# Weights of v in layer 0: high part by casting loads, low part by adding loads, for units 2 to 15

## The chip, the cores and the metric

The kernel runs on one core of one Trainium2 chip. The metric is the device time of the whole program in microseconds (us). Before the change it is 1315.11 us, the median of three runs (1314.94 to 1315.18).

## What is computed

A two-layer encoder step for 512 prompt rows and 8 x 16 sample rows, 640 token rows of 1024 in all, in float32. Layer 0 is a gated MLP, layer 1 an attention with forgetting. What the change touches is one product of layer 0, the v part of the input projection:

```python
h = rms_norm(x, norm_pre[0])                 # 640 x 1024
proj = h @ gmlp_w_in[0]                      # 1024 x 6144: u | v | z, 2048 columns each
uv = gelu(proj[..., :4096]); z = proj[..., 4096:]
v = layer_norm(uv[..., 2048:], ln_g, ln_b)
s = einsum('gij,bnjgc->bnigc', masked_w_s, v) + b_s
y = u * s * silu(z)                          # then y @ w_out, norms, embeddings, layer 1
```

## The kernel before

**Split operands.** TensorE multiplies in a reduced float32 form (fp32r). To keep float32 accuracy each operand is held as two fp32r parts, high = the rounded value and low = value minus high, and each product is three matmuls (`mm3`, lines 258 to 260): high by high, high by low, low by high. `split` makes the two parts: ScalarE copies into the high part (line 272), VectorE subtracts it from the source for the low part (line 273).

**Units of weights.** All weights of the program are cut into units of 512 KB, in the order of use. A unit of v is 256 rows by 512 columns: two blocks of 128 x 512. The 2048 columns of v are four panels p of 512 columns, each with four units kk (256 of the 1024 rows each), so units 0 to 15 are the weights of v and unit 4p + kk belongs to panel p. `fetch` loads a unit into one of three RAW buffers by a DMA on SyncE's queue (SP); `prefetch` gives each unit one of five slots of the tile W (2048 numbers per partition: 1024 high, 1024 low), splits it there and so fills W as far ahead as free slots allow. A slot is free again when TensorE has used its unit with all five token tiles. `weights(n)` hands out the next units and prefetches.

**The v stage.** For each panel five PSUM banks collect the five token tiles t (128 rows each); each unit is multiplied with the five tiles (5 x 2 x 3 = 30 matmuls of 128x512). At a panel's end ScalarE applies gelu (line 460) and VectorE takes statistics (line 461). After panel 3 the stage of u and z follows, whose units go through other sums (`left_operands`, line 200, on GpSimd, POOL in the profile).

**The start.** Ten loads bring the 640 token rows x; for each tile ScalarE squares one half (line 380), VectorE the other (381), VectorE adds (384, 280), GpSimd takes the power -0.5 (`rstd_of`, line 282), VectorE scales the rows (388), TensorE transposes them (296) and `split` writes the tile A, TensorE's other operand. Meanwhile units 0 to 4 are fetched and split.

**What sets the order.** The kernel is written with a tile framework whose scheduler orders each engine's instructions by its own timeline; each engine then runs its list strictly in order, and an instruction that waits for a semaphore holds all behind it on that engine. A DMA issued by GpSimd stands in GpSimd's list like any instruction. Semaphores come from the data that instructions read and write.

Of the kernel before, what the change touches and what calls it, by code (L numbers as in the profile page):

```python
# [19 lines left out]
AF = mybir.ActivationFunctionType  # L20
ALU = mybir.AluOpType
# [36 lines left out]
def hybrid_trunk(tc, x_prompt, x_sample, ck, cv, clf, p_prompt, p_sample, norm_pre, norm_post,  # L58
                 g_win, ln_g, ln_b, w_s, b_s, g_wout, f_win, b_f, f_wout, w_proj, w_gate, consts,
                 y_p, y_s, st_v, fk_p, fv_p, fl_p, fk_s, fv_s, fl_s):  # L60
    nc = tc.nc
# [28 lines left out]
    def r1(o, n, p=P):  # L90
        return R1[:p, o:o + n]

    def f(ap):
        return ap.bitcast(F32)
# [8 lines left out]
    def bank(lst=(0, 1, 2, 3, 4, 5, 6, 7)):  # L103
        return PB[ring(("bank", lst), lst)]
# [13 lines left out]
    def dma(out, in_):  # L118
        behind["sp"] = nc.sync.dma_start(out=out, in_=in_)
# [10 lines left out]
    units = []  # L130
# [12 lines left out]
    def u_tail(wout, layer):  # L143
        for h in range(2):
            for kk in range(8):
                u_rows(wout[0], kk * 256, h * 512, 2, 512)
        for h in range(2):
            u_rows(w_proj[layer], 0, h * 512, 2, 512)
        for h in range(2):
            for kk in range(4):  # L150
                u_rows(w_gate[layer], kk * 256, h * 512, 2, 512)

    u_tail(g_wout, 0)
    joined = set()
    for p in range(8):
        for part in (2, 1, 0, 3):
            for kk in range(2):
# [18 lines left out]
    state = {"raw": 0, "used": 0}  # L176

    def raw_of(i):
        if S0 <= i < S1:
            z = (i - S0 + 1) % 4  # L180
            if z == NRAW:
                return r1(o_X, 1024)
        else:
            z = i % NRAW if i < S0 else (i + 1) % NRAW
        return RAW[:, z * 1024:z * 1024 + 1024]

    def fetch(upto):
        while state["raw"] < min(upto, len(units)):
            ap, k = units[state["raw"]]
            dma(raw_of(state["raw"]).rearrange("p (k n) -> p k n", k=k), ap)  # L190
            state["raw"] += 1

    def left_operands(i, j):

        (a11, a21), (a12, a22) = ([raw_of(r).rearrange("p (k n) -> p k n", k=4)[:, :, z:z + P] for z in (0, P)] for r in (i, i + 1))
        s2, s3, s1, s4 = (SF[:, z * 512:z * 512 + 512].rearrange("p (k n) -> p k n", k=4) for z in range(4))
        if j == 0:
            for o, a, b, op in ((s1, a21, a22, ALU.add), (s2, s1, a11, ALU.subtract), (s3, a11, a21, ALU.subtract),
                                (s4, a12, s2, ALU.subtract)):
                nc.gpsimd.tensor_tensor(out=o, in0=a, in1=b, op=op)  # L200
        return (a11, SF[:, :1024], SF[:, 1024:2048], raw_of(i + 1))[j]

    def prefetch(upto, i0=0):

        while len(place) < min(upto, len(items)):
            i = len(place)
            u, j = items[i]
            taken = {z for k in range(i0, i) for z in place[k]}
            step = 1 if j == 0 else 2
            free = [z for z in range(0, 2 * (NW - (u in few)), step) if not taken & set(range(z, z + step))]  # L210
            if not free:
                return
            z = min(free, key=lambda z: max(last_use[z:z + step]))
            place.append(range(z, z + step))
            last_use[z:z + step] = [i] * step
            fetch(u + 1 if j is None else u + 2)
            o, n = z * 1024, step * 512
            hi, lo = W[:, o:o + n], W[:, o + n:o + 2 * n]
            if u in joined:
                k = units[u][1]  # L220
                hi, lo = (W[:, o:o + 2 * n].rearrange("p (k z n) -> p z k n", z=2, k=k)[:, z] for z in range(2))
                split(hi, lo, raw_of(u).rearrange("p (k n) -> p k n", k=k))
            elif j is None:
                split(hi, lo, raw_of(u))
            else:
                split(*((x.rearrange("p (k n) -> p k n", k=4) for x in (hi, lo)) if j == 0 else (hi, lo)), left_operands(u, j))
                if u > S0:
                    fetch(u + 4)

    def weights(n):  # L230

        i0 = state["used"]
        state["used"] += n
        prefetch(i0 + 2 * NW, i0)
        res = []
        for i in range(i0, i0 + n):
            u, j = items[i]
            k, o, m = units[u][1], place[i][0] * 1024, len(place[i]) * 512
            if u in joined:
                res.append(W[:, o:o + 2 * m].rearrange("p (k n) -> p k n", k=k))  # L240
                continue
            if j in (1, 2):
                views = [W[:, o + z:o + z + m].rearrange("p (a k n) -> p k a n", a=2, k=k) for z in (0, m)]
            else:
                views = [W[:, o + z:o + z + m].rearrange("p (k n) -> p k n", k=k) for z in (0, m)]
            res.append(tuple(views))
        return res
# [22 lines left out]
    def split(hi, lo, src):  # L270

        nc.scalar.activation(out=hi, in_=src, func=AF.Copy)  # L272
        nc.vector.tensor_tensor(out=lo, in0=src, in1=f(hi), op=ALU.subtract)  # L273
# [77 lines left out]
    def r2(o, n, p=P):  # L351
        return R2[:p, o:o + n]
# [13 lines left out]
    for i in range(N_WARM):  # L366
        nc.tensor.matmul(PB[7][:, :256], warm[:, :P], warm[:, 256:], start=True, stop=True)
    fetch(1)
    for t in range(1, NT):
        for h in range(2):  # L370
# [6 lines left out]
    for t in range(NT):  # L377
        x, xn = r2(t * D, D), r2(5120 + (t % 2) * D, D)
        ss = [small(), small()]
        nc.scalar.activation(out=xn[:, :512], in_=x[:, :512], func=AF.Square, accum_out=ss[0])  # L380
        nc.vector.scalar_tensor_tensor(out=xn[:, 512:], in0=x[:, 512:], scalar=1.0, in1=x[:, 512:], op0=ALU.mult, op1=ALU.mult,
                                       accum_out=ss[1])
        sq = small()
        nc.vector.tensor_tensor(out=sq, in0=ss[0], in1=ss[1], op=ALU.add)
        rs = rstd_of(sq, RMS_EPS)
        for h in range(2):
            hs = slice(h * 512, (h + 1) * 512)
            nc.vector.scalar_tensor_tensor(out=xn[:, hs], in0=x[:, hs], scalar=rs, in1=gb[h], op0=ALU.mult, op1=ALU.mult)
        transposed_split(xn, lambda c: h_hi[:, 4 * c:4 * c + 4, t * P:(t + 1) * P],
                         lambda c: h_lo[:, 4 * c:4 * c + 4, t * P:(t + 1) * P], (5, 6, 7))  # L390
        prefetch(t + 1)
# [51 lines left out]
    for p in range(4):  # L443
# [3 lines left out]
        out = [bank((0, 1, 2, 3, 4, 5, 6, 7)) for _ in range(NT)]  # L447
        for kk in range(4):
            (w,) = weights(1)
            for t in range(NT):  # L450
                for j in range(2):
                    k = 2 * kk + j
# [318 lines left out]
    n = NT * H  # L771
# [55 lines left out]
    scale = DH ** -0.5  # L827
# [343 lines left out]
```

## Time and profile before

| | |
|---|---|
| Median of three runs | 1315.11 us |
| Profiled execution | 1315.17 us, its span (first to last instruction) 1313.4 us |
| TensorE busy | 1304.7 us, 99% of the span |
| VectorE, ScalarE, GpSimd busy | 794.1, 553.1, 136.1 us |
| Mean granted TensorE clock | 0.997 of full speed |
| HBM read, written | 149.86 MB, 21.59 MB |
| v stage: last gelu of panels 0, 1, 2, 3 starts | 45.14, 71.89, 99.86, 127.43 us |

Times in the rows are microseconds from the first instruction. In a row of the timeline stand start, length, engine, line, operation, what it writes and reads, and in brackets how long the engine had been idle and what ended that. SPq and POOLq are the queues of DMA issues of SyncE and GpSimd.

### The profile page before, as it was taken

How to read it: one execution, taken by the hardware profiler on the slowest of the kernel's cores; microseconds unless marked ns; L12 is line 12 of the kernel's file. 1: busy time of each engine (PE TensorE's matmuls, PEld its weight loads, DVE VectorE, ACT ScalarE, POOL GpSimd, SP SyncE). 2: the span in 40 equal slices, each digit the busy share in tenths (PEclk: the TensorE clock that was granted, in tenths of full speed). 3: DMA queues.
4: the chain of work that ended last, by engine and by line, in shares of the span. 5: the costliest groups of instructions: out<-in, count | busy, mean ns of one | idle time of the engine just before them, and what ended most of it. 6: DMA issues, size and time to landing. Idle time of an engine off the chain costs nothing.

```text
span 1313.4 us, 20355 instructions
## 1 busy us (share of the span) xinstructions
PE 1304.7 (99%) x7683; PEld 1152.3 (88%) x7683; DVE 794.1 (60%) x1671; ACT 553.1 (42%) x1074; POOL 136.1 (10%) x144
## 2 busy tenths in 40 slices
PE   8999999999999999999999999999999999999998
PEld 6888999999988888888999889898988988888887
DVE  7744999999844455644555554556555566554543
ACT  5334555444535343533433334333434344435431
POOL 1012454543000000000000000000000000000100
PEclk8999999999999999999999999999999999999999
DMA  6432333232424213589676665788557687343211
GB/s 227 132 108 67 120 118 121 86 104 73 129 94 149 79 49 113 167 135 149 152 194 151 155 160 148 165 150 171 132 150 163 149 213 235 113 132 132 66 56 57
DMA packets 300053, 172.79 MB, mean 132 GB/s; under 512 B 188785, under 2 KB 269473, under 8 KB 299954
## 3 DMA queue, kind: packets, MB, share of 16 engines
q1 hardware_dynamic: 299810, 171.23, 49.3%
q8 instruction: 60, 0.98, 0.3%
q14 instruction: 39, 0.32, 0.1%
q10 hardware_dynamic: 144, 0.26, 0.1%
HBM read 149.86 MB, written 21.59 MB: 131 GB/s over the span
## 4 chain that ended last, share of the span: by engine, by line
PE 95%; DVE 3%; DMA 1%; issue 1%; ACT 0%; SPq 0%; POOL 0%; DVEq 0%
PE pb L258 22%; PE pb L260 22%; PE pb L259 22%; PE pb L324 7%; PE pb L867 6%; PE pb L325 3%; PE pb L868 3%; PE pb L986 3%; PE pb L979 1%; PE pb L1040 1%; PE pb L1066 1%; PE pb L296 1%; DVE W L273 1%; PE pb L571 1%; PE pb L1063 1%
## 5 line engine op out<-in xcount | busy, mean ns | idle before, releaser
L273 DVE TENSOR_TENSOR W<-RAW,W 128x1024 fp32r<-128x1024 f32 (+1 forms) x156 | 193.5, 1242 | 170.8 <-ACT W L272 136.5
L272 ACT ACTIVATE W<-RAW 128x1024 fp32r<-128x1024 f32 (+1 forms) x156 | 161.0, 1033 | 151.0 <-PE pb L260 47.5
L258 PE MATMUL pb<-A,W 128*128 128x384 f32 (+1 forms) x640 | 221.8, 347 | 0.0
L260 PE MATMUL pb<-A,W 128*128 128x384 f32 (+1 forms) x640 | 208.7, 326 | 0.0
L259 PE MATMUL pb<-A,W 128*128 128x384 f32 (+1 forms) x640 | 208.3, 325 | 0.0
L258 PE MATMUL pb<-W,A 128*128 128x512 f32 x520 | 205.0, 395 | 2.3 <-ACT A L272 2.3
L259 PE MATMUL pb<-W,A 128*128 128x512 f32 x520 | 203.7, 392 | 0.0
L260 PE MATMUL pb<-W,A 128*128 128x512 f32 x520 | 203.3, 393 | 0.1
L324 PE MATMUL pb<-A,W 128*128 128x512 f32 x384 | 150.7, 393 | 0.0
L258 PEld LDWEIGHTS pb<-A,W 128*128 128x128 f32 x640 | 120.4, 188 | 18.7 <-issue 8.9
L259 PEld LDWEIGHTS pb<-A,W 128*128 128x128 f32 x640 | 121.0, 189 | 0.7
L260 PEld LDWEIGHTS pb<-A,W 128*128 128x128 f32 x640 | 120.2, 188 | 0.1
L258 PEld LDWEIGHTS pb<-W,A 128*128 128x128 f32 x520 | 98.1, 189 | 22.3 <-ACT A L272 2.5
L867 PE MATMUL pb<-W,A 128*128 128x512 f32 x320 | 116.6, 403 | 0.0
L260 PEld LDWEIGHTS pb<-W,A 128*128 128x128 f32 x520 | 97.9, 188 | 20.9 <-DVE A L273 0.6
L259 PEld LDWEIGHTS pb<-W,A 128*128 128x128 f32 x520 | 98.0, 188 | 19.4
L325 PE MATMUL pb<-A,W 128*128 128x256 f32 x384 | 107.7, 280 | 0.0
L868 PE MATMUL pb<-W,A 128*128 128x256 f32 x320 | 89.5, 280 | 0.0
L273 DVE TENSOR_TENSOR A<-R,A 128x640 fp32r<-128x640 f32 (+1 forms) x51 | 41.0, 836 | 71.4 <-ACT A L272 70.7
L867 PEld LDWEIGHTS pb<-W,A 128*128 128x128 f32 x320 | 60.0, 188 | 15.1 <-DVE R L872 2.6
L325 PEld LDWEIGHTS pb<-A,W 128*128 128x128 f32 x384 | 72.1, 188 | 0.4 <-issue 0.4
L324 PEld LDWEIGHTS pb<-A,W 128*128 128x128 f32 x384 | 72.1, 188 | 0.2
(252 smaller groups left out, 2285.8 us busy)
## 6 DMA issues: line engine op xcount, KB each, us to landing
RAW<-in_fox_w_in SPq DMA_DIRECT2D x64, 512.0 KB
RAW<-in_gmlp_w_in SPq DMA_DIRECT2D x40, 512.0 KB
r2b_t<-in_cache_fox_v SPq DMA_DIRECT2D x32, 512.0 KB
r2b_t<-in_cache_fox_k SPq DMA_DIRECT2D x128, 128.0 KB
RAW<-in_gmlp_w_out SPq DMA_DIRECT2D x16, 512.0 KB
RAW<-in_ple_w_gate SPq DMA_DIRECT2D x16, 512.0 KB
RAW<-in_fox_w_out SPq DMA_DIRECT2D x16, 512.0 KB
out<-R SPq DMA_DIRECT2D x42, 128.0 KB
```

Of the source, the lines that this page charges most:

```text
L258: nc.tensor.matmul(out, lh, rh, start=start, stop=False)
L259: nc.tensor.matmul(out, lh, rl, start=False, stop=False)
L260: nc.tensor.matmul(out, ll, rh, start=False, stop=stop)
L272: nc.scalar.activation(out=hi, in_=src, func=AF.Copy)
L273: nc.vector.tensor_tensor(out=lo, in0=src, in1=f(hi), op=ALU.subtract)
L296: nc.tensor.transpose(out=b[:, j * P:(j + 1) * P], in_=src[:, (4 * c + j) * P:(4 * c + j + 1) * P], identity=ident)
L324: nc.tensor.matmul(out[1].rearrange("p (z n) -> p z n", z=2), w[0], h_both[:, :, k, SA:], start=k == 0, stop=False)
L325: nc.tensor.matmul(out[1][:, :TOK - SA], w[1], h_hi[:, k, SA:], start=False, stop=k == 7)
L571: nc.tensor.matmul(b0[:, t * P:(t + 1) * P], v_at(pnl, t)[:, c0:c0 + P], wm, start=True, stop=True)
L867: nc.tensor.matmul(b, hi, w, start=k == 0, stop=False)
L868: nc.tensor.matmul(b[:, :256], lo, w[:, :256], start=False, stop=k == 7)
L986: nc.tensor.matmul(O[:, d], v[:, j, hh * P:(hh + 1) * P], pt[:, j * P:(j + 1) * P], start=(j == 0), stop=(j == i))
```

## The change

For units 2 to 15 `fetch` loads nothing into RAW. Instead `prefetch` issues a load from GpSimd that goes straight from the weights in HBM to the unit's high half in W, cast to fp32r on the way; ScalarE writes the negative of the high part into the low half; a second load from GpSimd reads the same weights again and adds them to the low half. Units 0 and 1, and all from 16 on, are split as before. So 14 loads of 512 KB on SP's queue, 14 copies on ScalarE and 14 subtractions on VectorE (128x1024 each) go; 28 loads of 512 KB on GpSimd's queue and 14 negating copies on ScalarE (128x1024) come.

```diff
-    joined = set()
+    joined, by_dma = set(), set(range(2, 16))
...
     def fetch(upto):
         while state["raw"] < min(upto, len(units)):
+            if state["raw"] in by_dma:
+                state["raw"] += 1
+                continue
             ap, k = units[state["raw"]]
...
                 split(hi, lo, raw_of(u).rearrange("p (k n) -> p k n", k=k))
+            elif u in by_dma:
+                src, k = units[u]
+                hi, lo = (x.rearrange("p (k n) -> p k n", k=k) for x in (hi, lo))
+                nc.gpsimd.dma_start(out=hi, in_=src)
+                nc.scalar.activation(out=lo, in_=f(hi), func=AF.Copy, scale=-1.0)
+                nc.gpsimd.dma_start(out=lo, in_=src, accum_op=ALU.add)
             elif j is None:
                 split(hi, lo, raw_of(u))
```

The change shifts line numbers by 9 behind the new code: line 282 is 291 in the changed kernel, 380 is 389, 272 is 281, 499 is 508; line 200 is 203. The new lines are 229 (casting load), 230 (negation) and 231 (adding load).

GpSimd at the start, before (line 282 is the power; the row ISA ahead of it selects GpSimd's library; line 499 clears two blocks; line 200 is `left_operands`):

```order
L1167 UNCONDITIONAL_BRANCH
L282 ISA
L282 TENSOR_TENSOR SML<-SML 128x1 x5
L499 MEMSET R_69 64x64 x2
L200 TENSOR_TENSOR sf<-RAW 128x512 x2
L200 TENSOR_TENSOR sf<-sf,RAW 128x512
```

And now:

```order
L1176 UNCONDITIONAL_BRANCH
L229 DMA W<-in_gmlp_w_in 128x2x512 x3
L231 DMA W<-in_gmlp_w_in 128x2x512
L291 ISA
L291 TENSOR_TENSOR SML<-SML 128x1
L231 DMA W<-in_gmlp_w_in 128x2x512 x2
L291 TENSOR_TENSOR SML<-SML 128x1 x4
```

The casting loads of units 2, 3 and 4 stand first, the adding load of unit 2 ahead of the power of tile 0, and those of units 3 and 4 ahead of the power of tile 1.

ScalarE at the start, before (line 380 squares a tile of x, line 272 copies a high part, into W for a weight and into A for a transposed tile):

```order
L380 ACT_TABLE_LOAD
L380 ACTIVATE r2a_t,SML<-r2a_t 128x512
L272 ACTIVATE W<-RAW 128x1024
L380 ACTIVATE r2a_t,SML<-r2a_t 128x512
L272 ACTIVATE A<-pb_75 128x4x128
L380 ACTIVATE r2a_t,SML<-r2a_t 128x512
L272 ACTIVATE W<-RAW 128x1024
L272 ACTIVATE A<-pb_76 128x4x128
```

And now:

```order
L230 ACT_TABLE_LOAD
L230 ACTIVATE W<-W 128x1024
L389 ACTIVATE r2a_t,SML<-r2a_t 128x512
L230 ACTIVATE W<-W 128x1024
L281 ACTIVATE W<-RAW 128x1024
L281 ACTIVATE A<-pb_75 128x4x128
L389 ACTIVATE r2a_t,SML<-r2a_t 128x512
L281 ACTIVATE A<-pb_76 128x4x128
L230 ACTIVATE W<-W 128x1024
```

The negation of unit 2 stands ahead of the first square, that of unit 3 ahead of the split of unit 0, and that of unit 4 behind both halves of tile 0. On TensorE 9 matmuls and 20 transposes now stand ahead of the first matmul that needs the low part of unit 1 (before, 7 and 16); from unit 5 on its order is the same in both.

GpSimd further on, now (before, only line 200 and the two clears stood there): units 5, 6, 7, then 8, 9, 10 and so on to 15.

```order
L203 TENSOR_TENSOR sf<-RAW 128x512 x2
L203 TENSOR_TENSOR sf<-sf,RAW 128x512
L203 TENSOR_TENSOR sf<-RAW,sf 128x512
L229 DMA W<-in_gmlp_w_in 128x2x512 x3
L231 DMA W<-in_gmlp_w_in 128x2x512 x3
L229 DMA W<-in_gmlp_w_in 128x2x512
L231 DMA W<-in_gmlp_w_in 128x2x512
L229 DMA W<-in_gmlp_w_in 128x2x512
L231 DMA W<-in_gmlp_w_in 128x2x512
```

From unit 8 on each unit's adding load stands between its own casting load and that of the next unit; ahead of unit 5's stand the four sums of the first unit of u, which wait for the last tile of x since they reuse its memory.

## The prediction

> **What bounds the kernel now.** First I read the chain that ended last, by engine, then the busy time of each engine in stretches of the v stage, then the timeline rows at the places the change touches.
>
> ```profile
> PE 95%; DVE 3%; DMA 1%; issue 1%; ACT 0%; SPq 0%; POOL 0%; DVEq 0%
> core 0: us, PE busy (x) PEld busy (x) DVE busy (x) ACT busy (x) POOL busy (x), PEclk, DMA share, GB/s
> 5.10:8.50 3.40, 2.23 (x8) 0.79 (x6) 0.90 (x2) 1.02 (x2) 0.56 (x1) 1.00 0.96 324
> 8.50:11.90 3.40, 2.00 (x7) 1.28 (x7) 3.23 (x7) 2.16 (x7) 0.02 (x1) 0.50 1.04 402
> 11.90:15.40 3.50, 3.50 (x14) 2.91 (x13) 2.93 (x4) 1.34 (x3) 0.53 (x1) 0.51 1.06 398
> 15.40:20.00 4.60, 4.47 (x22) 3.39 (x21) 4.57 (x11) 4.04 (x7) 0.95 (x1) 1.00 0.68 257
> 20.00:45.20 25.20, 25.20 (x125) 20.98 (x124) 16.50 (x27) 11.49 (x18) 1.47 (x2) 1.00 0.30 93
> 45.20:99.90 54.70, 54.70 (x242) 44.90 (x241) 36.14 (x33) 19.29 (x27) 6.25 (x6) 1.00 0.44 131
> 99.90:127.50 27.60, 27.60 (x125) 22.96 (x125) 10.94 (x22) 8.68 (x13) 6.87 (x8) 1.00 0.23 77
> ```
>
> TensorE is the bound. From 20 to 127.5 us it is busy without a gap; no weight is waited for there, and what the change takes from VectorE and from SP's queue shortens nothing. Only before 15.4 us is there loss: TensorE waits, and its granted clock is 0.5 from 8.5 to 15.4 us, while the DMA engines are full (about 400 GB/s). So a gain can come from the first 15 us alone, a loss from anything that is late for TensorE. Its pace is read from the last gelu of each panel:
>
> ```profile
> 45.14 0.60 ACT L460 ACTIVATE R<-pb 128x512 f32<-128x512 f32 x1 [0.76 <-PE pb L260]
> 51.54 1.06 ACT L272 ACTIVATE W<-RAW 128x1024 fp32r<-128x1024 f32 x1 [4.85 <-PE pb L260]
> 127.43 0.58 ACT L460 ACTIVATE R<-pb 128x512 f32<-128x512 f32 x1
> ```
>
> Panel 0 ends at 45.1, panel 3 at 127.4 us: 82.3 us for 12 units, 6.86 us a unit (0.229 us a matmul). The row at 51.54 is a split that waits for TensorE to free unit 4's slot, so unit 5 is needed at 51.5 us, unit n at 51.5 + 6.86 (n - 5), unit 15 at 120.1 us.
>
> **The start, step by step.** The rows of before:
>
> ```profile
> 2.03 0.43 SPq L119 DMA_DIRECT2D RAW<-in_gmlp_w_in  x1
> 3.50 0.63 ACT L380 ACTIVATE r2a_t<-r2a_t 128x512 f32<-128x512 f32 x1 [1.08 <-DMA r2a_t<-in_x_prompt]
> 4.04 0.19 ACT L380 ACTIVATION_READ_ACCUMULATOR r2a_t<-r2a_t 128x1 f32 x1
> 4.91 0.16 DVE L384 TENSOR_TENSOR SML<-SML 128x1 f32<-128x1 f32 x1
> 5.34 0.56 POOL L282 TENSOR_TENSOR SML<-SML 128x1 f32<-128x1 f32 x1 [4.90 <-DVE SML L280]
> 5.93 0.75 DVE L388 SCALAR_TENSOR_TENSOR r2a_t<-r2a_t,SML,pb 128x512 f32<-128x512 f32 x1 [0.68 <-POOL SML L282]
> 7.48 1.06 ACT L272 ACTIVATE W<-RAW 128x1024 fp32r<-128x1024 f32 x1 [3.26 <-DMA RAW<-in_gmlp_w_in]
> 8.57 1.23 DVE L273 TENSOR_TENSOR W<-RAW,W 128x1024 fp32r<-128x1024 f32 x1 [1.89 <-ACT W L272]
> 9.68 0.79 PE L258 MATMUL pb<-W,A 128*128 128x512 f32 x1 [2.29 <-ACT A L272]
> 11.88 0.56 POOL L282 TENSOR_TENSOR SML<-SML 128x1 f32<-128x1 f32 x1 [5.98 <-DVE SML L280]
> 13.79 1.22 DVE L273 TENSOR_TENSOR W<-RAW,W 128x1024 fp32r<-128x1024 f32 x1
> 15.53 0.48 PE L259 MATMUL pb<-W,A 128*128 128x512 f32 x1
> 29.64 0.87 PE pb L296 x8
> 88.48 12.81 SPq L119 DMA_DIRECT2D RAW<-in_gmlp_w_in  x3
> 92.16 1.29 POOL L200 TENSOR_TENSOR sf<-RAW 128x512 f32<-128x512 f32 x1 [5.32 <-DMA RAW<-in_gmlp_w_in]
> ```
>
> *Landing of a load of 512 KB:* issued at 88.48 on quiet DMA engines it lets its reader start at 92.16, 3.7 us; issued at 2.03 among the loads of x it lands by 7.48, 5.4 us. No load issued by GpSimd is in the trace; GpSimd is free at 0.44. The issue of one costs between SP's 0.43 us and the 1.29 us of GpSimd's own pass over 128x512; I take 1.0, since GpSimd must write out 256 rows of 2 KB in software, which resembles its pass more than SP's issue. The first casting load then lands between 4.5 and 6.5 us; I take 5.7.
>
> *Power of tile 0:* negation of unit 2 (1.06, as the copy of line 272) until 6.8; behind it the square (0.63 and 0.19, with the handing over 0.8) until 7.6 instead of 4.2; VectorE's two small operations 0.3: 7.9. GpSimd's adding load issues from 6.8 to 7.8, so the power stands from 7.9 to 8.5, not 5.3 to 5.9: 2.6 us late. The first matmul follows less late, since unit 0 held it before: a scaling (0.75), four transposes (0.7) and the copy into A (0.6, as line 460's of the same size) make about 10.5 for 9.68; the transposes of the second half end at 10.8.
>
> *Power of tile 1:* GpSimd comes to it only after the adding load of unit 4, which waits for the negation of unit 4, which on ScalarE stands behind both halves of tile 0: transposes end at 10.8, then square (0.8), second half (0.6), negation (1.06) make 13.3, issue 1.0, so the power starts at 14.4 for 11.88. VectorE then has four scalings (3.0) and the low part of unit 1 (1.23), done at 19.4 with the handing over, for 15.0. TensorE, in order, waits for it at 19.5 instead of 15.53. By then it has done 2 matmuls (0.46) and 4 transposes (0.87 for 8, so 0.44) more than before: 4.0 - 0.9 = **3.1 us lost**. Behind this point units 1 to 3 with three tiles (some 60 matmuls, 14 us) are ready, and tiles 3 and 4 come in time.
>
> *Clock:* it returned at 15.4, after a stretch of 3.4 us in which TensorE had no gap; in the one before, 2.00 of 3.40 busy, it stayed at 0.5. In the changed kernel the stretches to 15.4 and to 18.8 hold gaps, so I expect 22.2; from 19.5 on that is 2.7 us at half pace, **1.3 us lost** (0, if it returns at 18.8).
>
> **Units 5 to 15.** GpSimd's four sums of 1.29 us stand ahead of unit 5's casting load and wait for the last transposes (34.4 us before, with the rest of the stage shifted alike; I leave the shift out on both sides): 34.4 + 5.2 = 39.6. Three casting loads issue until 42.6; unit 5 lands at 44, negation until 45.3, its adding load issues until 46.3 and lands at 50, for 51.5: it holds, by 1.5 us. The three adding loads are out by 49.
>
> From unit 8 on GpSimd works a strict round: issue casting load, wait for it to land, wait for ScalarE's negation, issue adding load, only then the next unit. Its length R decides. Casting load 3.7 and 0.6 for the longer issue; 1.0 since the adding load of the unit before is still moving ahead of it (512 KB at the 400 GB/s of the windows are 1.3 us, part of it behind the issue); negation 1.06; 0.3 for a gelu that ScalarE has just begun (0.60, half the time); issue 1.0: R = 7.7 us. That is above TensorE's 6.86, so GpSimd falls behind, but it starts with a lead: unit 15 is ready at 49 + 8 R + 4 (last landing) = 114.6, needed at 120.1. The rounds fit up to R = 8.4; **0 us lost** at my value, 8 us for each us beyond. Bounds of R: 5.2 (3.7, 1.06, issue 0.43, nothing between) and 11.5 (issue 1.29 twice, negation 1.06, gelu 0.60, and a load's 3.7 plus 2.6 to 3.6 when an adding load, which must read its target too, moves at half or a third of the pace). With 11.5 the loss is 25 us.
>
> The Trainium skill bears on R twice. Its page "DMA: Bandwidth & Descriptors", section "Anatomy of one DMA — SWDGE (gpsimd) path", gives about 2.0 us plus bytes over 436 GB/s for a load issued by GpSimd: an estimate of 3.2 us for 512 KB, R 7.2 and still no loss; no run here shows it yet. Against the change speak the next rows:
>
> ```profile
> 93.98 1.92 DVE L273 TENSOR_TENSOR W<-RAW,W 128x1024 fp32r<-128x1024 f32 x1 [5.53 <-ACT W L272]
> 94.89 2.15 POOL L200 TENSOR_TENSOR sf<-RAW,sf 128x512 f32<-128x512 f32 x1
> ```
>
> A GpSimd pass of the same size takes 2.15 us here and 1.29 at 92.16, and the split that VectorE had begun at 93.98 takes 1.92 for 1.23. If the issues stretch by this 0.86 too, R is 9.4 and 8 us are lost. The page "SBUF — State Buffer", section "Who interferes with whom", says that such a VectorE operation on two tiles holds up GpSimd's reads and that writing descriptors, by inference, only needs the write side: by that rule the issues don't stretch; the row agrees as far as reads go.
>
> **What goes.** 14 subtractions of 1.23 us and 14 copies of 1.06 on VectorE and ScalarE (the copies return as negations), 7.3 MB on SP's queue: hidden under TensorE's gapless 20 to 127 us, so 0. The second read of 7.3 MB fits: DMA share 0.30 to 0.44 there. Should the cast not round, the low parts are near zero and accuracy goes, not time.
>
> **Sum.** 1315.17 us (span 1313.4 and 1.8 around it; 0.06 over the median) + 3.1 + 1.3 + 0 = **1319.6 us**. The start alone has bounds: casting load at 4.5 and issue 0.43 make some 1.5 us with no clock loss; at 6.5 and 1.29 and a second stretch at half clock, 8.
>
> **Rivals.**
> 1. *GpSimd's round is the bound* (R from 9.4 to 11.5): the start's 4.4 and 8 to 25 us, 1328 to 1345. For it: strict order, two issues and a landing in each round, R close to the edge. Against it: the lead of 5.5 us, and half-empty DMA engines.
> 2. *Not slower.* VectorE is nearly full from 8.5 to 20 us (3.23 of 3.40, 2.93 of 3.50, 4.57 of 4.60), and the splits of units 2, 3, 4 leave it (3.7 us). If unit 2 lands by 4.5 and the issue is cheap, the power of tile 0 is only 1.4 late, the tiles follow more densely, the clock returns at 15.4 as before. TensorE's gaps from 8.5 to 20 are 1.5 us, so this gives 1313.7 to 1317. Against it: unit 0 still lands at 7.5, and the power waits whatever VectorE does.
> 3. *GpSimd's library.* Before, it is selected at the start, in GpSimd's 4.90 us of idle time, and no row shows its cost, between 0 and 4.6; now it stands behind the first adding load and ahead of the power. Fully paid: 1319.6 + 4.6 = 1324.
>
> **How the numbers follow.** The forecast (start late, rounds just fit; 1317 to 1324) gets 0.50, rival 1 0.27, rival 2 0.14, rival 3 0.09. About 0.2% (2.6 us) is what a measurement can tell from no change: 1312.5 to 1317.7 is "same". Of rival 2, 0.03 lies below, 0.10 within, 0.01 above; of the forecast's low end 0.02 lies within. Faster 0.03, same 0.12, slower 0.85. The range leaves out most of rival 2's lower half and rival 1's upper half: 1316.5 to 1338; the forecast's own is 1317 to 1324.
>
> **What would show it.** Right: the first power on GpSimd near 8 us, the first square near 7, half clock beyond 15.4, no gap on TensorE from 22 to the end of panel 3, adding loads landing a few us ahead of use. Wrong in the rounds: TensorE idle for loads of W from unit 8 on, growing unit by unit, and GpSimd's queue stepping at more than 8.4 us. Wrong in the start: the first power at 6 us or above 12. Wrong altogether: gaps after 130 us.

## The result: 1.35% slower, and the profile after

| | before | changed |
|---|---|---|
| Median | 1315.14 us (4 runs, 1314.94 to 1315.20) | 1332.60 us (4 runs, 1331.92 to 1334.37) |
| Profiled execution, its span | 1315.17, 1313.4 us | 1332.96, 1331.2 us |
| TensorE's first matmul of 512 columns | 9.68 us | 15.17 us |
| Start of matmul 200 | 51.3 us | 58.1 us (+6.8) |
| Start of matmul 400 | 96.76 us | 113.74 us (+17.0) |
| Start of matmul 7600 | 1295.5 us | 1312.9 us (+17.4) |

The ratio is 1.0135, 95% interval 1.0118 to 1.0153. Matmuls are counted in the order of the trace, transposes among them. Nearly all of the 17.5 us is lost at two places: 6.8 us before 47 us and 10.2 us between 81 and 100 us. Behind that the two traces run in parallel. The stretches of the changed kernel (columns: length, then busy time and count of TensorE, its weight loads, VectorE, ScalarE and GpSimd, then granted clock, DMA share, GB/s):

```profile
10.00:15.00 5.00, 1.63 (x8) 1.57 (x8) 2.75 (x5) 3.38 (x6) 3.15 (x3) 1.00 1.11 384
15.00:20.00 5.00, 2.85 (x8) 1.77 (x6) 4.01 (x13) 3.82 (x8) 2.30 (x3) 1.00 1.11 270
20.00:25.00 5.00, 4.92 (x21) 4.14 (x22) 5.00 (x10) 2.56 (x6) 0.00 (x0) 0.66 1.10 267
45.00:80.00 35.00, 35.00 (x155) 28.72 (x154) 18.86 (x16) 12.39 (x14) 9.23 (x11) 1.00 0.79 176
80.00:90.00 10.00, 4.84 (x20) 3.31 (x19) 1.29 (x2) 2.03 (x3) 1.95 (x2) 0.95 0.71 133
90.00:100.00 10.00, 6.93 (x25) 5.45 (x26) 5.27 (x5) 2.52 (x4) 1.95 (x2) 0.70 0.57 128
100.00:145.00 45.00, 45.00 (x204) 37.46 (x203) 14.82 (x26) 16.41 (x26) 16.00 (x15) 1.00 0.54 122
```

**The start.** ScalarE, GpSimd, VectorE and TensorE in the timeline of the changed kernel:

```profile
9.23 1.06 ACT L230 ACTIVATE W<-W 128x1024 fp32r<-128x1024 f32 x1 [6.80 <-DMA W<-in_gmlp_w_in]
10.19 0.61 ACT L389 ACTIVATE r2a_t<-r2a_t 128x512 f32<-128x512 f32 x1
12.88 1.04 ACT L281 ACTIVATE W<-RAW 128x1024 fp32r<-128x1024 f32 x1
...
1.25 2.38 POOL L229 DMA_DIRECT2D W<-in_gmlp_w_in  x3 [0.81 <-POOLq L1167]
10.60 1.23 POOL L231 DMA_DIRECT2D W<-in_gmlp_w_in  x1 [6.96 <-ACT W L230]
11.46 1.07 POOL L291 TENSOR_TENSOR SML<-SML 128x1 f32<-128x1 f32 x1
18.51 1.25 POOL L291 TENSOR_TENSOR SML<-SML 128x1 f32<-128x1 f32 x2
...
21.92 1.22 DVE L282 TENSOR_TENSOR W<-RAW,W 128x1024 fp32r<-128x1024 f32 x1
...
15.17 0.79 PE L267 MATMUL pb<-W,A 128*128 128x512 f32 x1
```

The first casting load issues at 1.25 and lands at 9.2 us. Until then ScalarE stands at the negation (line 230) with the first square behind it, and so the power of tile 0 comes at 11.46 us (5.34 before), the first real matmul at 15.17. The power of tile 1 follows at 18.51 (11.88 before) and the low part of unit 1 at 21.92 (13.79 before); TensorE comes to the first matmul that needs it at 23.35 (15.53 before).

**The stall at 81 to 93 us.** What TensorE waited for between 50 and 145 us (us in total, times, longest):

```profile
PE pb L267 <- ACT R L469: 8.2, 2, 6.9
```

The timeline rows of TensorE at these waits, of ScalarE ahead of them, and of GpSimd:

```profile
83.19 0.50 PE L267 MATMUL pb<-W,A 128*128 128x512 f32 x1 [1.37 <-ACT R L469]
93.07 0.79 PE L267 MATMUL pb<-W,A 128*128 128x512 f32 x1 [6.85 <-ACT R L469]
...
72.27 1.06 ACT L230 ACTIVATE W<-W 128x1024 fp32r<-128x1024 f32 x1 [8.03 <-DMA W<-in_gmlp_w_in]
81.60 1.06 ACT L230 ACTIVATE W<-W 128x1024 fp32r<-128x1024 f32 x1 [5.94 <-issue]
82.56 1.07 ACT L469 ACTIVATE R<-pb 128x512 f32<-128x512 f32 x2
91.48 1.06 ACT L230 ACTIVATE W<-W 128x1024 fp32r<-128x1024 f32 x1 [7.84 <-DMA W<-in_gmlp_w_in]
92.44 1.55 ACT L469 ACTIVATE R<-pb 128x512 f32<-128x512 f32 x3
...
63.37 1.19 POOL L231 DMA_DIRECT2D W<-in_gmlp_w_in  x1 [8.12 <-ACT W L230]
64.11 1.22 POOL L229 DMA_DIRECT2D W<-in_gmlp_w_in  x1
73.63 1.19 POOL L231 DMA_DIRECT2D W<-in_gmlp_w_in  x1 [8.31 <-ACT W L230]
83.69 1.22 POOL L229 DMA_DIRECT2D W<-in_gmlp_w_in  x1
128.85 1.19 POOL L231 DMA_DIRECT2D W<-in_gmlp_w_in  x1 [6.98 <-ACT W L230]
```

TensorE does not wait for weights. It waits for a PSUM bank, and the gelu that would empty it (line 469) stands on ScalarE behind the negation of unit 11, which waits until 91.5 us for a casting load issued at 83.69. After the wait of 6.85 us the clock is at half for a while (0.70 from 90 to 100 us): six matmuls take 2.7 us instead of 1.4, so 1.4 of the 10.2 us are the clock. Behind the waits stand GpSimd's rounds: from the adding load of unit 8 (63.37) to that of unit 15 (128.85) they take 65.48 / 7 = **9.35 us each**, where TensorE uses a unit in 6.86.

So there are two theories for the second loss. **Theory A**: the round of 9.35 us is the cause, and the loss is charged wherever something first runs dry. **Theory B**: the gelus behind waiting negations are the cause, and without them the lead would cover the rounds.

### The profile page after: what moved, and what is told of

It reads as the page before. It is cut to its first block, busy times and chain, and to the rows that moved or that the text cites. A ratio compares the mean times of both kernels' runs of the same rounds, so it can differ in the third digit from the quotient of the medians.

```text
span 1331.2 us, 20365 instructions
## 1 busy us (share of the span) xinstructions
PE 1309.0 (98%) x7683; PEld 1154.3 (87%) x7683; DVE 778.3 (58%) x1657; ACT 550.9 (41%) x1074; POOL 165.1 (12%) x172
## 4 chain that ended last, share of the span: by engine, by line
PE 91%; issue 3%; DVE 3%; DMA 2%; POOL 1%; ACT 1%; POOLq 0%; DVEq 0%
PE pb L267 21%; PE pb L269 20%; PE pb L268 20%; PE pb L333 7%; PE pb L876 6%; PE pb L334 3%; PE pb L877 3%; PE pb L995 3%; PE pb L988 1%; PE pb L1049 1%; PE pb L1075 1%; DMA W<-in_gmlp_w_in 1%; PE pb L305 1%; PE pb L580 1%; DMA RAW<-in_gmlp_w_in 1%
## 5 line engine op out<-in xcount | busy, mean ns | idle before, releaser
L282 DVE TENSOR_TENSOR W<-RAW,W 128x1024 fp32r<-128x1024 f32 x142 | 176.7, 1246 | 147.2 <-ACT W L281 115.3
L281 ACT ACTIVATE W<-RAW 128x1024 fp32r<-128x1024 f32 x142 | 146.1, 1031 | 118.0 <-PE pb L333 40.2
```

## Experiments: start and rounds, each alone

Edit of the first: `by_dma = set(range(5, 16))`; of the second: `by_dma = set(range(2, 5))`.

> Only units 5 to 15 by loads that cast and add; units 2 to 4 are split as before the change. Theory A (GpSimd's round of 9.35 us against TensorE's 6.86 us a unit sets the loss behind 80 us): the start's 6.8 us goes, but GpSimd's first casting load of these units waits for the last transposes, which move forward by only some 3.5 us, while TensorE moves forward by 6.8; so the lead is about 3 us shorter and the loss in the rounds grows from 10 to about 13 us: 1326 to 1329 us, rounds still 9 to 9.5 us, first matmul of 512 columns near 9.7 us. Rival (the two losses simply add): 1332.6 - 6.8 = 1325.8 us. Rival (the late start causes both): no loss, 1315.

Measured: 1327.26 us (1326.15 to 1328.06), ratio 1.0089 (1.0072 to 1.0106). Matmul 200 stands 0.3 us earlier than before, matmul 400 11.5 later: the loss in the rounds grew from 10.2 to 11.8 us. That is the direction theory A gives, with a little less than its 13; simple adding, 1325.8, lies below all four runs. But theory A's reason for the growth is not what the traces show. Unit 15's adding load lands at 127.73 us here and at 135.07 in the changed kernel. TensorE needed that unit at 120.11 before; shifted by what each kernel has lost up to matmul 200 (-0.3 and 6.8 us), the load is 7.9 us late here and 8.2 there, so by this estimate the rounds alone cost much the same. The rest of the loss, 3.9 and 2.0 us, comes from TensorE being stopped earlier, at the held gelus, with the slow clock behind that: it uses the low part of unit 15 only at 131.61 and 137.09, that much after the landing. The wait has another name:

```profile
PE pb L445 <- DVE R L442: 8.1, 1, 8.1
```

Line 445 transposes the sums of the spatial weights, which VectorE (line 442) makes behind the statistics of panel 1, and these wait for the same gelus. The round is unchanged: adding loads from 55.53 to 121.62 us, 9.44 us each.

> Only units 2 to 4 by loads that cast and add. If the start's delay stands by itself: matmul 200 stands 6.8 us later than before, nothing is lost behind it, 1315.1 + 6.8 to 7.2 = 1322 us. If half of it is due to what comes after (the order of the list changes when the later units go back): 1319 to 1320, the size of my forecast for the start alone.

Measured: 1322.28 us (1321.87 to 1323.05), ratio 1.0053 (1.0038 to 1.0068); matmul 200 is 7.5 us late, matmul 7600 is 7.6. The start's loss stands by itself.

## Experiments: which cause in the rounds

**Negations of units 5 to 15 on VectorE.**

```diff
-                nc.scalar.activation(out=lo, in_=f(hi), func=AF.Copy, scale=-1.0)
+                if u < 5:
+                    nc.scalar.activation(out=lo, in_=f(hi), func=AF.Copy, scale=-1.0)
+                else:
+                    nc.vector.tensor_scalar(out=lo, in0=f(hi), scalar1=-1.0, scalar2=None, op0=ALU.mult)
```

> As the changed kernel, but the negations of units 5 to 15 run on VectorE, so no gelu stands behind a negation that waits for a load. Theory A (the round sets the loss, its place is of no account): the wait for PSUM banks at 81 to 93 us goes, and TensorE waits for W instead, for units 12 to 15: unit 15's adding load still issues at about 129 us and lands at 135, needed at 127: 8 us late, and 0 to 2 us for the clock; 1328 to 1332 us. Theory B (the gelus held on ScalarE are the cause): rounds as long as before, but no stall, 1322 us.

Measured: 1327.73 us (1326.19 to 1328.77), between the theories' numbers. The banks' wait is gone, as both theories said, but TensorE does not wait for W as theory A said; it waits 4.6 us for the sums of the spatial weights, as in the kernel of the rounds alone, now behind a negation on VectorE itself. The list also came out differently (two casting loads in a row for units 8 and 9), so that the round is 8.7 us (63.15 to 124.27). The run does not decide: whichever engine has the negations, something of the program stands behind them.

**Strict rounds, but no gelu behind a waiting negation.** The pieces of units 10 and 11 are issued behind the gelus of panel 1, those of 14 and 15 behind those of panel 2, and each casting load stays behind the adding load before it:

```diff
-                nc.gpsimd.dma_start(out=hi, in_=src)
-                nc.scalar.activation(out=lo, in_=f(hi), func=AF.Copy, scale=-1.0)
-                nc.gpsimd.dma_start(out=lo, in_=src, accum_op=ALU.add)
+                def piece(hi=hi, lo=lo, src=src, u=u):
+                    with ExitStack() as stack:
+                        if u > 7:
+                            stack.enter_context(tc.issue_after(behind["add"].ins))
+                        nc.gpsimd.dma_start(out=hi, in_=src)
+                    with ExitStack() as stack:
+                        if u in (10, 11, 14, 15):
+                            stack.enter_context(tc.issue_after(behind["act"].ins))
+                        nc.scalar.activation(out=lo, in_=f(hi), func=AF.Copy, scale=-1.0)
+                    behind["add"] = nc.gpsimd.dma_start(out=lo, in_=src, accum_op=ALU.add)
+                if u in (10, 11, 14, 15):
+                    held.append(piece)
+                else:
+                    piece()
...
+        while p in (1, 2) and held:
+            held.pop(0)()
```

> As the changed kernel, with GpSimd's strict order kept, but the negations of units 10 and 11 stand on ScalarE behind the gelus of panel 1, those of units 14 and 15 behind the gelus of panel 2: no gelu waits for a load. Theory A (the round of 9.3 us against 6.86 us costs some 8 to 10 us wherever it is charged): no wait for a PSUM bank; TensorE waits for W in units 12 to 15 instead, unit 15's adding load issues at about 129 us, lands at 135, needed at 127: 1328 to 1331 us. Theory B (the gelus behind the negations are the cause): no gap, 1322 us.

Measured: 1332.36 us (1331.54 to 1333.61): no faster than the changed kernel's 1332.60. Now TensorE waits for weights (line 280 is the second matmul of the three, high by low, the first that needs a unit's low part). Its waits for them from 5 to 140 us:

```profile
PE pb L280 <- DMA W<-in_gmlp_w_in: 7.3, 5, 2.8
```

The rows of the timeline at which the low parts of units 12 to 15 are first used:

```profile
110.30 0.73 PE L280 MATMUL pb<-W,A 128*128 128x512 f32 x1 [2.78 <-DMA W<-in_gmlp_w_in]
119.27 0.50 PE L280 MATMUL pb<-W,A 128*128 128x512 f32 x1 [0.28 <-DMA W<-in_gmlp_w_in]
128.83 0.50 PE L280 MATMUL pb<-W,A 128*128 128x512 f32 x1 [2.46 <-DMA W<-in_gmlp_w_in]
137.53 0.50 PE L280 MATMUL pb<-W,A 128*128 128x512 f32 x1 [1.61 <-DMA W<-in_gmlp_w_in]
```

They stand 9 us apart: GpSimd's pace. Theory B gave 1322 and falls; theory A holds, 1 us above its range. That the time is the same as the changed kernel's is partly chance, though: the rounds are longer here (adding loads of units 8 to 15 from 63.41 to 131.58, 9.74 us each for 9.35), so unit 15 lands 2.4 us later, at 137.49, and this makes up for the 2.0 us that the held gelus and the clock behind them cost in the changed kernel. So of its 10.2 us some 8 are the rounds, wherever they are booked, and some 2 the gelus behind waiting negations.

**What makes the round long: a plain second load.** For units 5 to 15 `accum_op=ALU.add` is left out of the second load, which then writes over the negative, so the kernel leaves out the subtraction and its low part is the whole weight.

> As the changed kernel, but for units 5 to 15 the second load writes over the negative instead of adding to it (low part wrong, same bytes read). Theory C (the adding load moves at half the pace, 2.85 us for 512 KB against 1.3, and the next casting load waits behind it): plain second loads take 1.3 us, the casting load lands 5.5 us after its issue instead of 8, the round falls to 7 to 7.7 us, the lead covers it: 1322 us. Rival (any second load behind the first in GpSimd's list costs the same): round 9.3 us, 1332 us.

Measured: 1323.41 us (1321.81 to 1324.79); in its trace TensorE has no wait behind the start, and matmul 400 is as late as matmul 200 (5.8 us). GpSimd's rounds, with the negations between:

```profile
60.18 0.72 POOL L234 DMA_DIRECT2D W<-in_gmlp_w_in  x1 [7.56 <-ACT W L230]
60.89 0.72 POOL L229 DMA_DIRECT2D W<-in_gmlp_w_in  x1
67.05 0.72 POOL L234 DMA_DIRECT2D W<-in_gmlp_w_in  x1 [5.45 <-ACT W L230]
109.91 0.72 POOL L234 DMA_DIRECT2D W<-in_gmlp_w_in  x1 [5.86 <-ACT W L230]
...
65.69 1.06 ACT L230 ACTIVATE W<-W 128x1024 fp32r<-128x1024 f32 x1 [4.05 <-DMA W<-in_gmlp_w_in]
```

The round is (109.91 - 60.18) / 7 = 7.1 us, with the same list and the same bytes read from HBM. The casting load behind a plain load lands 4.8 us after its issue (60.89 to 65.69); behind an adding load, in the changed kernel, it took 8.2 (64.11 to 72.27), and over its seven rounds 7.25 on average. So adding, not reading twice, makes the difference of 2.2 us in each round.

The traces also show where the time goes. The last second load of each kernel has no casting load behind it. From its issue to its landing the adding load takes 6.2 us (changed kernel, from 128.85), the plain one 4.0 (from 109.91). GpSimd's DMA queue in these two stretches, the adding load first (packets, MB, share of the time of 16 engines):

```profile
q0 software_dynamic: 272, 0.52, 55.1%
...
q0 software_dynamic: 272, 0.52, 47.5%
```

The packets are as many and as large, but the stretches are 6.3 and 4.1 us long, so a packet takes some 0.20 us with adding and 0.11 without (an estimate from the two rows). While the adding load moves (132.5 to 133.5 us) the engines are full, a share of 1.13, at 207 GB/s; a plain load and the casting load behind it (98 to 99.5 us) fill them, a share of 1.15, at 367 GB/s.

**Half the units.** `by_dma = set(range(5, 16, 2))`.

> Only units 5, 7, 9, 11, 13 and 15 by loads that cast and add; the others are split. Theory A (GpSimd's round against TensorE's pace): a round of 9 to 10 us now has two units, 13.7 us, to fit in, so no gap on TensorE from 20 to 130 us: 1315 to 1316 us. Theory B (a gelu or a reduction behind a negation that waits for a load, whatever the pace): a gap of 1 us or more at a panel's end, 1317 us or more.

Measured: 1315.84 us, ratio 1.0004 (0.9995 to 1.0014), TensorE without a gap from 20 to 130 us. Two units per round are enough, and six loads less on SP's queue and six subtractions less on VectorE bring nothing.

**All units from 5 on, the order of two issues turned round.** Each casting load goes ahead of the adding load of the unit before:

```diff
-                nc.gpsimd.dma_start(out=hi, in_=src)
+                cast = nc.gpsimd.dma_start(out=hi, in_=src)
+                if held:
+                    with tc.issue_after(cast.ins):
+                        held.pop()()
                 nc.scalar.activation(out=lo, in_=f(hi), func=AF.Copy, scale=-1.0)
-                nc.gpsimd.dma_start(out=lo, in_=src, accum_op=ALU.add)
+                held.append(lambda lo=lo, src=src: nc.gpsimd.dma_start(out=lo, in_=src, accum_op=ALU.add))
+                if u == 15:
+                    held.pop()()
```

> As units 5 to 15 alone, but each unit's casting load is issued ahead of the adding load of the unit before, so that GpSimd no longer waits for a landing and a negation between two issues. Theory A: the round disappears (issues 0.74 + 1.2 us, paced by W's slots, 6.86 us), the casting load runs without an adding load just ahead of it, lands 5 us after its issue, so no gelu is held and no unit late: 1315 to 1316 us. Rival (the bandwidth or the half pace of the adding loads is the bound, not the order): the loss stays, 1322 to 1327 us.

Measured: 1316.53 us, ratio 1.0010 (1.0000 to 1.0019), half a microsecond above theory A's range; against the same units in strict rounds (1327.26) 10.7 us are won by order alone. GpSimd's longest wait from 50 to 135 us:

```profile
POOL W L230 <- PE pb L275: 22.9, 6, 5.3
```

Two of its steps in the timeline (line 230 is the casting load, 235 the adding load):

```profile
79.73 0.74 POOL L230 DMA_DIRECT2D W<-in_gmlp_w_in  x1 [5.26 <-PE pb L275]
80.45 1.24 POOL L235 DMA_DIRECT2D W<-in_gmlp_w_in  x1
86.68 0.74 POOL L230 DMA_DIRECT2D W<-in_gmlp_w_in  x1 [4.99 <-PE pb L275]
```

GpSimd now waits for TensorE to free slots (line 275 is the third matmul), 7 us a step, instead of TensorE for GpSimd. The rival, that the bandwidth of the adding loads is the bound, falls: at 7 us a unit they fit.

## Experiments: what is slow in the start

In both, `by_dma = set(range(2, 5))`. The first:

```diff
                 nc.gpsimd.dma_start(out=hi, in_=src)
-                nc.scalar.activation(out=lo, in_=f(hi), func=AF.Copy, scale=-1.0)
-                nc.gpsimd.dma_start(out=lo, in_=src, accum_op=ALU.add)
+                with tc.issue_after(squares[(2, 2, 3)[u - 2]].ins):
+                    nc.scalar.activation(out=lo, in_=f(hi), func=AF.Copy, scale=-1.0)
+                with tc.issue_after(powers[(1, 1, 2)[u - 2]].ins):
+                    nc.gpsimd.dma_start(out=lo, in_=src, accum_op=ALU.add)
```

> Only units 2 to 4 by loads that cast and add, as in e2, but on ScalarE their negations stand behind the squares of tile 2 (unit 4: tile 3), and on GpSimd the adding loads behind the power of tile 1 (unit 4: tile 2). Theory S1 (the start's loss is order: the first square behind a negation that waits 8 us for its load, the power behind an adding load): first matmul of 512 columns back at 9.7 us, power of tile 0 at 5.5, 1315 to 1317 us. Theory S2 (the loads of GpSimd take the DMA engines from x, unit 0 and unit 1): loss stays, first matmul after 12 us, 1319 to 1322 us.

Measured: 1320.21 us (1319.58 to 1320.52), ratio 1.0038; matmul 200 is 4.5 us late, for 7.5 in the start alone. Both theories take a part: the power of tile 0 is back at 5.50 us, but the first matmul comes at 12.03, because unit 0 itself lands late. ScalarE's first square and its copy of unit 0:

```profile
3.55 0.63 ACT L392 ACTIVATE r2a_t<-r2a_t 128x512 f32<-128x512 f32 x1 [1.12 <-DMA r2a_t<-in_x_prompt]
10.44 1.06 ACT L284 ACTIVATE W<-RAW 128x1024 fp32r<-128x1024 f32 x1 [6.16 <-DMA RAW<-in_gmlp_w_in]
```

Before, this copy stood at 7.48. The second takes the first's edit and also puts the casting loads behind the power of tile 0:

```diff
-                nc.gpsimd.dma_start(out=hi, in_=src)
+                with tc.issue_after(powers[0].ins):
+                    nc.gpsimd.dma_start(out=hi, in_=src)
```

> As e8 (units 2 to 4 alone, negations and adding loads behind squares and powers), but the three casting loads issue behind the power of tile 0, at about 6.1 us instead of 1.25. Theory S2 (what is left of the start's loss, 4.5 us, is that GpSimd's 1.5 MB of early loads take the DMA engines from unit 0 and from tiles 1 and 2 of x): unit 0 is copied near 7.5 us again, not 10.4, first matmul near 9.7, half of the 4.5 us or more goes: 1315.5 to 1317.5 us. Rival (the second reads, 1.5 MB more in the first 30 us, cost it whenever they come): stays at 1319 to 1321 us.

Measured: 1316.93 us (1316.54 to 1317.41), ratio 1.0013 (1.0004 to 1.0023):

```profile
5.75 2.37 POOL L231 DMA_DIRECT2D W<-in_gmlp_w_in  x3
7.12 1.06 ACT L285 ACTIVATE W<-RAW 128x1024 fp32r<-128x1024 f32 x1 [3.02 <-DMA RAW<-in_gmlp_w_in]
```

Unit 0 is in time, the first matmul at 9.86, matmul 200 0.6 us late. By the medians, of the start's 7.0 us, 2.1 go with the order (1322.28 to 1320.21) and 3.3 with the later casting loads (to 1316.93); the DMA engines are full at that time in any case (a share of 1.06 from 11.9 to 15.4 us before the change). Some 1.7 us remain; no run here shows their cause.

**Both mended, all 14 units.**

> All units 2 to 15 by loads that cast and add, as in the changed kernel, with both orders mended: the start as in e9, each casting load from unit 6 on issued ahead of the adding load of the unit before as in e6. If order was the whole cause of the loss in the rounds and start and rounds are independent: the time of e9 plus 0.3 to 1.2 us, 1316 to 1318.5 us, no gap on TensorE from 50 to 130 us. If the two together bring back a loss: 1320 us or more.

Measured: 1318.25 us (1317.66 to 1319.16), ratio 1.0024 (1.0014 to 1.0034): the time as expected at its upper end, but not without gaps:

```profile
PE pb L458 <- DVE R L455: 1.2, 1, 1.2
PE pb L280 <- ACT R L482: 0.9, 1, 0.9
```

The edit is that of the later casting loads for units 2 to 4 and of the turned order from unit 5 on. In the trace GpSimd's clearing of two blocks, which stands ahead of unit 11's casting load, waits for VectorE until 72.64 us (65.72 with the turned order alone), so that load issues at 73.17 instead of 66.26, and the negation at 78.07 us, which waits for it, still holds gelus and the reductions behind them. 14.4 of the 17.5 us are recovered by the order and time of issue alone. No version with these loads was faster than the kernel before.

## Why the prediction was right or wrong, step by step

**Right: direction, the wide range, and what bounds the kernel. Wrong: the forecast itself.** The measured 1332.60 us is 13.0 above the forecast of 1319.6 and outside its own 1317 to 1324; it lies in the range of 1316.5 to 1338 only because that takes in half of rival 1. TensorE is the bound, and work taken from SP and VectorE brings nothing (every other unit: 1.0004). Right too: unit 5 holds (TensorE is without a gap from 45 to 80 us), and nothing is lost behind 130 us.

**The start: the chain was right, its first term too small.** 4.4 us were forecast (3.1 and 1.3 for the clock), 6.8 came, within the bound of 8. "The first casting load then lands between 4.5 and 6.5 us; I take 5.7": it landed at 9.2, outside the bounds and 3.5 us late. The rest of the chain keeps about that distance: the power of tile 0 at 11.46 for 7.9, that of tile 1 at 18.51 for 14.4, the low part of unit 1 done at 23.1 for 19.4. The issue cost 0.8 us (2.38 for three, for my 1.0), so that is no cause. The prediction had seen that the DMA engines are full then, but it priced the load by one that shares them with x alone (5.4 us) and left out that three casting loads, 1.5 MB, come on top: these land at 9.2, 11.9 and 14.8 us. The first takes 8 us whether it issues at 1.25 or, in the last kernel of the start, at 5.75 (negation at 14.01), and at 1.25 the three of them delay unit 0's copy by 3 us (7.48 to 10.44). From trace to trace the loss follows this landing: 8.4 us in that of the plain second loads, where matmul 200 is 5.8 us late, 9.2 and 6.8 in the changed kernel's, 10.4 and 7.5 in that of the start alone. The clock's 1.3 us are not settled. The clock is at half for some 3.4 us of the stretch from 20 to 25 us (0.66, so the estimate), later than forecast; in the kernel with the start alone no window from 5 to 25 us is below 1.00, but its load also landed 1.2 us later, so the two cannot be set against each other.

**The rounds: the term that failed.** R was put at 7.7 us: casting load 4.3, **1.0 for the adding load ahead of it**, negation 1.06, 0.3, issue 1.0. Measured: 9.35, of which the casting load from its issue 7.25 (for 4.3 + 1.0), negation 1.06, handing over 0.3, and 0.74 from one issue to the next. The quiet casting load was rightly sized: issued at 38.52 it lands by 42.94 in the kernel with turned order, 4.4 us. So the queue term was 2.9 us (7.25 less 4.4), not 1.0: it was taken for 512 KB at 400 GB/s, and the adding load moves at 207 GB/s and lands 6.2 us after its issue. I had the right figure among my bounds ("half or a third of the pace") and chose the low end, though that was the one row the trace did not have. The Trainium skill, "DMA: Bandwidth & Descriptors", section "Anatomy of one DMA — SWDGE (gpsimd) path", gives 2.0 us plus bytes over 436 GB/s, an estimate of 3.2 us for this load; here the nearest row has 4.4, and its rule has no term for a load that adds. With R as measured the prediction's own rule, 8 us for each us beyond 8.4, gives 7.6 us; by the landing of unit 15 the rounds cost 8.2, and 10.2 came with the held gelus and the clock behind them.

**The place was missed altogether.** "What would show it" named TensorE idle for loads of W, growing unit by unit. In the changed kernel there were two waits for PSUM banks, since I asked what stands behind GpSimd's waits and not what stands behind ScalarE's: the negation waits for a load, and the gelus of panel 1 are queued behind it. The kernel with the gelus ahead shows the forecast picture. So most of the size, some 8 of 10.2 us, follows from the round; the place, and some 2 us more, from the order.

**The rivals.** The first, GpSimd's round as the bound, is what happened, with R at its low end (9.4) and the time inside its 1328 to 1345. I gave it 0.27 and the fitting round 0.50; an edge of 0.7 us (7.7 against 8.4), resting on one unmeasured term of 1.0, did not carry that preference. Its feared cause did not occur: the issues of the changed kernel did not stretch. An adding load's issue takes 1.19 to 1.23 us throughout; a casting load's takes 0.71 to 0.92, and up to 1.22 right behind an adding load, where it begins 0.74 us after it. The Trainium skill's page "SBUF — State Buffer", section "Who interferes with whom", infers that writing descriptors is not held up by VectorE's operations on two tiles; the issues agree: the adding load at 63.37 us takes 1.19 us beside two such operations (from 62.45 and 63.86), and the one at 111.13 takes 1.19 with none. *GpSimd's library*: the power of tile 0 takes 1.07 us for 0.56, half a microsecond, not 4.6. *Not slower*: with order and time of the start's loads mended, and the splits of units 2 to 4 off VectorE, the kernel still took 1.7 us more than before, so the relief of VectorE did not pay for the rest.

## What to carry to other kernels

When one engine issues two dependent loads for each piece of work, write down its round as a chain, and price the second load by what it does to the first load of the next round: here the order of two issues was worth 10.7 us with the same loads. An instruction that waits for a load on an in-order engine holds whatever the program needs behind it (here a negation held the gelus until 92.44 us), so list that for every engine on which the change adds a wait, and do not take the wait that the profile names for the cause until a run without it is faster. A term that no row prices, on which the verdict turns, deserves the high bound as much as the low one.

## What the runs showed of the hardware

An adding load of 512 KB moves at little more than half the pace of plain and casting ones from GpSimd: 207 GB/s for 367 with the DMA engines equally full (shares of 1.13 and 1.15). The trace shows as many packets for it as for a plain load (272), so none in smaller pieces; alone it lands 6.2 us after its issue, a plain one 4.0. It delays a casting load behind it by some 2.2 us more than a plain load of the same bytes (7.25 against about 5 us from issue to landing). Its issue row is 1.2 us long, that of a plain load 0.72. Whether it is the reading of the target that makes it slow, no run here shows.
